# Two weight chunks first in the load queue of the first feature group

## The chip, the cores and the metric

The kernel runs on one core of one Trainium2 chip, in float32, in one launch. The metric is the device time in microseconds (us); the lower, the better. A core has TensorE (PE, matmuls; its loads of stationary operands are listed as PEld), VectorE (DVE), ScalarE (ACT), GpSimd (POOL) and SyncE (SP), which here only issues DMA transfers. They run side by side and wait for each other through semaphores.

## The reference

One layer of a decoder is computed for 288 tokens: 256 of a prompt and 8 requests of 4 tokens. `c` holds nine conditioning vectors, one for the prompt and one for each request.

```
mod = silu(c) @ w_ada + b_ada            # (9, 6 * 2048): sh1, sc1, g1, sh2, sc2, g2
h = rmsnorm(x, norm1) * (1 + sc1) + sh1
proj = h @ w_in                          # 2048 -> u_pool, z, xbc, dt
...                                      # pooling mixer, Mamba-2 mixer
x = x + g1 * (concat(pool_out, ssd_out) @ w_out)
h2 = rmsnorm(x, norm2) * (1 + sc2) + sh2
...                                      # gated MLP with a causal convolution
x = x + g2 * ffn_out
```

The change touches only the first part: `sh1` and `sc1`, the normalised and modulated input `h`, and the columns of the projection that are computed first.

## The kernel before

Features lie on the 128 partitions, tokens on the free axis (N = 288). The 2048 input features are KT = 16 feature tiles of 128.

**Feature groups.** The first projection can't start before `h` exists, and `h` needs `sh1` and `sc1`, a product with 2 x 2048 columns of `w_ada`. The kernel therefore splits the input features into six groups, `KGROUPS`, of 1, 1, 2, 4, 4 and 4 feature tiles (groups 0 to 5). For each group it first makes the conditioning (`ada_group_units`): 4, 4, 8, 16, 16 and 16 loads of 512 KB (`raw_ada`), which small matmuls consume in batches of four loads (tile `adag`), a copy on ACT (`asb_g`), a transposing matmul (`adat_g`), an addition on DVE (`ada`). Then `modulate` makes `h` for these feature tiles (`h_g`), casts it on ACT to a rounded high part (`h1h`, L368) and subtracts on DVE to a low part (`h1l`, L369).

**The projection.** `xbc_units(gi)` then adds this group's share to all ET = 28 output tiles, numbered `m` (i in the loop below). Its weights come in chunks of 512 KB (`raw_xbc`; the last chunk of groups 0 and 1 has 256 KB): 4, 4, 7, 14, 14 and 14 chunks in groups 0 to 5. A chunk holds 8 output tiles in groups 0 and 1, 4 in group 2, and 2 in groups 3 to 5. `split` casts a chunk on ACT to the high part `whi` (L220) and subtracts on DVE for the low part `wlo` (L221); there are two buffers of each. Three matmuls (L226 to L228) make each product from high and low parts. The result leaves PSUM by copies on ACT in group 0 (L574) and is added by DVE in the later groups (L576); three PSUM buffers rotate.

**The order of loads.** `load` (L213) takes one of 16 `raw` buffers and issues the transfer on SP's queue. All weights go through this one queue in program order, and a load whose buffer is not free holds up the ones behind it. The engines' own order is set by the framework's scheduler at build time; SP's order in the trace is that of the program.

**Interleaving.** `next_groups` is a generator that yields after each conditioning load; the call after a batch's fourth load also issues the batch's matmuls, and the call after a group's last load also its `modulate`. Before the loop over groups, `AN[0]` = 5 calls are made: group 1's four loads, and then group 1's matmuls and `modulate` with the first load of group 2. In the loop, `pull` adds a rate after each output tile and makes a call for each whole unit of credit:

```
    for _ in range(AN[0]):
        next(nxt)
...
        for i, m in enumerate(xbc_units(gi)):
            if not last:
                pull(nxt, AN[gi + 1] / (ET - 4))
```

A chunk's load stands where `xbc_units` reaches it, unless it is in `ready` already (before: only chunk 0 of group 0). `vec` (L895) is a table that is loaded at the start of group 1.

Of the kernel before, what the change touches and what calls it, by code (L numbers as in the profile page):

```python
# [35 lines left out]
ET = XT + len(UEARLY) + 3 * ZEARLY  # L36
# [4 lines left out]
YK = 2  # L41
AQ = (4, 4, 4, 4, 4, 4)

AN = (5, 5, 7, 11, 14, 15)
AY = 2

RA1, RA2, RB1, RB2, RB3 = 0.5, 0.4, 1.0, 1.0, 1.0
# [86 lines left out]
def kernel(ctx: ExitStack, tc, ins, outs):  # L134
# [75 lines left out]
    def load(key):  # L210
        off, cols = S.items[key]
        t = wp[0].tile([P, RAWC], F32, tag="raw", name="raw_" + "_".join(map(str, key)))
        nc.sync.dma_start(t[:, :cols], wflat[off:off + P * cols].rearrange("(p n) -> p n", p=P))  # L213
        return t

    def split(raw, a, n, name, urgent=True):
        hi = wp[0].tile([P, RAWC], F32R, tag="whi", name="whi_" + name)
        lo = wp[0].tile([P, RAWC], F32R, tag="wlo", name="wlo_" + name)
        with tc.high_priority() if urgent else nullcontext():
            nc.scalar.copy(hi[:, :n], raw[:, a:a + n])  # L220
            nc.vector.tensor_tensor(lo[:, :n], raw[:, a:a + n], hi[:, :n].bitcast(F32), ALU.subtract)  # L221
        return hi, lo

    def mm3(ps, whi, wlo, c, bh, bl, first, last, n=P):
        w = slice(c * n, c * n + n)
        nc.tensor.matmul(ps, whi[:, w], bh, start=first, stop=False)  # L226
        nc.tensor.matmul(ps, whi[:, w], bl, start=False, stop=False)  # L227
        nc.tensor.matmul(ps, wlo[:, w], bh, start=False, stop=last)  # L228

    ready = {}  # L230
# [223 lines left out]
    def late_loads():  # L454
        nc.vector.tensor_copy(selr, seli)
        nc.vector.tensor_scalar(csr, vec[:, K_TRI:K_TRI + N], 0.0, None, ALU.mult)

    def late_states():
        nc.sync.dma_start(poolw, ins["pool_w"])
        st = sx[0].tile([P, XT * NB * 3 + 4 * NB * 15], F32, tag="cf", name="st", bufs=2)  # L460
        nc.sync.dma_start(st, ins["st"])
        n = XT * NB * 3
        for g in range(4):
            nc.gpsimd.tensor_copy(cvs(g)[:, :, :, 0:3], st[:, 0:n].rearrange(
                "p (g m b l) -> p g m b l", g=4, m=5, b=NB)[:, g])
        nc.gpsimd.tensor_copy(ups.rearrange("p m b l -> p (m b) l")[:, :, 0:15],
                              st[:, n:].rearrange("p (m l) -> p m l", l=15))
# [86 lines left out]
    def xbc_units(gi):  # L554
        k0, gk = KGROUPS[gi]
        for ci, (ks, ms) in enumerate(_xbc_chunks(gi)):
            hi, lo = split(ready.pop(("xbc", gi, ci), None) or load(("xbc", gi, ci)), 0, len(ms) * gk * P, f"xbc{gi}_{ci}",
                           gi + 1 == len(KGROUPS))
            for b, m in enumerate(ms):
                ps = pm.tile([P, 512], F32, tag="mm", name=f"xbc{gi}_{m}")  # L560
                for i, k in enumerate(ks):
                    mm3(ps[:, :N], hi, lo, b * gk + i, xhi[0][k], xlo[0][k], i == 0, i == gk - 1)
                if m < XT:
                    g, r = divmod(m, 5)
                    parts = [(cvp[g][:, r, 3:3 + NP], ps[:, 0:NP]), (cvs(g)[:, r, :, 3:7], samp(ps[:, NP:N]))]
                elif m < XT + len(UEARLY):
                    u = UEARLY[m - XT]
                    parts = [(upp[:, u, 15:], ps[:, 0:NP]), (ups[:, u, :, 15:19], samp(ps[:, NP:N]))]
                else:
                    g, t = divmod(m - XT - len(UEARLY), 3)  # L570
                    parts = [(zy[g][:, t, :], ps[:, 0:N])]
                for o, v in parts:
                    if gi == 0:
                        nc.scalar.copy(o, v)  # L574
                    else:
                        nc.vector.tensor_tensor(o, o, v, ALU.add)  # L576
                yield m

    def drain(gen):
        for _ in gen:  # L580
            pass
# [253 lines left out]
    def next_groups():  # L835
        for gi in range(1, len(KGROUPS)):
            k0, gk = KGROUPS[gi]
            yield from ada_group_units(gi)
            modulate(xav(k0, gk), rstd1, 0, 0, k0, gk, f"g{gi}")

    nxt = next_groups()
# [29 lines left out]
    def pull(gn, rate):  # L871

        credit[id(gn)] = credit.get(id(gn), 0.0) + rate
        while credit[id(gn)] >= 1:
            credit[id(gn)] -= 1
            next(gn, None)

    ready["xbc", 0, 0] = load(("xbc", 0, 0))
    for _ in range(AN[0]):
        next(nxt)  # L880
    for gi in range(len(KGROUPS)):
        last = gi + 1 == len(KGROUPS)
        if last:

            wp[0].drop(w0)
            w0_ctx.close()
            sx[0] = mx_ctx.enter_context(tc.tile_pool(name="sx", bufs=1, reuse_waits="tile"))
            hi, lo = split(load(("dt",)), 0, KT * NH, "dt")
            ps = pm.tile([P, 512], F32, tag="mm", name="mm_dt")
            for k in range(KT):  # L890
                mm3(ps[0:NH, :N], hi, lo, k, xhi[0][k], xlo[0][k], k == 0, k == KT - 1, NH)
            late_states()
            dt_stage(ps)
        elif gi == 1:
            nc.sync.dma_start(vec, ins["vec"])  # L895
        elif gi == 4:
            late_loads()
        for i, m in enumerate(xbc_units(gi)):
            if not last:
                pull(nxt, AN[gi + 1] / (ET - 4))  # L900
                if i == ET - 4 and gi == 4:
                    drain(nxt)
            else:
                pull(back, 0.5 if m < 20 else RB1) if m >= 9 else None
                pull(adas, RA1 / AY)
# [389 lines left out]
```

## Time and profile before

| | |
|---|---|
| median of 3 runs | 1383.16 us (1382.48 to 1385.14) |
| the profiled execution, its time | 1382.64 us |
| its span in the trace | 1380.9 us |
| mean granted TensorE clock | 0.993 |
| TensorE busy | 1357.1 us (98%) |
| DVE busy | 822.1 us (60%) |
| ACT busy | 575.8 us (42%) |
| moved by DMA | 323.20 MB |

The span runs from the first to the last instruction of the program in the trace; the execution's own time is 1.7 us longer. Busy is the time in which an engine works on an instruction; the granted clock is a share of full speed, where 1.00 is 2.4 GHz.

### The profile page before, as it was taken

Reading aid. Unit: us, or ns where it says so; the run is one execution under the profiler, and the core shown is the slowest. Engines: PE = TensorE matmul, PEld = TensorE weight load, DVE = VectorE, ACT = ScalarE, POOL = GpSimd, SP = SyncE. Lnnn points to the kernel's source line nnn. Section 1 sums busy time; section 2 is a strip of 40 time slices with the busy share of each in tenths; the row PEclk is TensorE's granted clock in tenths of the full one; section 3 lists DMA queues with packets and bytes.
Section 4 is the critical chain, followed back from the end, with each engine's and each line's share of the span. In section 5 each row is a group of like instructions: output and inputs, shape, how many; then the busy total and the mean of one; then the engine's idle time right before and its main releaser. Section 6 shows DMA issues by size and latency. Waiting matters only on the chain.

```text
span 1380.9 us, 26414 instructions
## 1 busy us (share of the span) xinstructions
PE 1357.1 (98%) x10557; PEld 1256.4 (91%) x10557; DVE 822.1 (60%) x1450; ACT 575.8 (42%) x925; POOL 222.8 (16%) x426
## 2 busy tenths in 40 slices
PE   7899999999999999999999999999999999999997
PEld 6789887776679898998999999999999999999997
DVE  3686667977674448655655545665555556565553
ACT  3432334378653334533443333444343333443452
POOL 0000001222222123111211001222120012122221
PEclk9999999999999999999999999999999999999998
DMA  9997876888788877788655555655555555665531
GB/s 373 357 341 287 309 261 255 316 297 298 271 330 320 323 277 254 234 275 290 205 179 180 166 169 184 202 191 186 182 181 161 177 193 188 198 187 193 187 119 69
DMA packets 97194, 323.20 MB, mean 234 GB/s; under 512 B 10736, under 2 KB 19888, under 8 KB 97072
## 3 DMA queue, kind: packets, MB, share of 16 engines
q1 hardware_dynamic: 93168, 310.63, 65.2%
q0 software_dynamic: 3184, 9.69, 1.9%
q8 instruction: 83, 1.36, 0.4%
q10 hardware_dynamic: 720, 1.19, 0.2%
q14 instruction: 39, 0.32, 0.1%
HBM read 309.78 MB, written 10.39 MB: 232 GB/s over the span
## 4 chain that ended last, share of the span: by engine, by line
PE 94%; DVE 3%; DMA 1%; ACT 1%; issue 1%; POOL 0%; SPq 0%; DVEq 0%; ACTq 0%; POOLq 0%
PE mm_down L226 7%; PE mm_down L228 7%; PE mm_down L227 7%; PE mm_gate L228 6%; PE mm_gate L226 6%; PE mm_val L227 6%; PE mm_gate L227 6%; PE mm_val L228 6%; PE mm_val L226 6%; PE adap L255 4%; PE xbc L226 4%; PE xbc L228 4%; PE xbc L227 4%; PE mm_out L226 3%; PE mm_out L227 2%; PE mm_out L228 2%
## 5 line engine op out<-in xcount | busy, mean ns | idle before, releaser
L226 PE MATMUL mm_down<-ah,whi_down 128*128 128x288 f32 x688 | 203.7, 296 | 0.0
L228 PE MATMUL mm_down<-ah,wlo_down 128*128 128x288 f32 x688 | 203.5, 296 | 0.0
L227 PE MATMUL mm_down<-al,whi_down 128*128 128x288 f32 x688 | 203.3, 295 | 0.0
L228 PE MATMUL mm_gate<-h2h,wlo_gate 128*128 128x288 f32 x640 | 190.2, 297 | 0.0
L226 PE MATMUL mm_gate<-h2h,whi_gate 128*128 128x288 f32 x640 | 189.8, 297 | 0.0
L227 PE MATMUL mm_gate<-h2l,whi_gate 128*128 128x288 f32 x640 | 189.3, 296 | 0.0
L227 PE MATMUL mm_val<-h2l,whi_val 128*128 128x288 f32 x640 | 188.8, 295 | 0.0
L228 PE MATMUL mm_val<-h2h,wlo_val 128*128 128x288 f32 x640 | 188.5, 295 | 0.0
L226 PE MATMUL mm_val<-h2h,whi_val 128*128 128x288 f32 x640 | 188.0, 294 | 0.0
L221 DVE TENSOR_TENSOR wlo_gate<-raw_gate,whi_gate 128x1024 fp32r<-128x1024 f32 x80 | 97.9, 1225 | 139.4 <-ACT whi_gate L220 139.3
L221 DVE TENSOR_TENSOR wlo_down<-raw_down,whi_down 128x1024 fp32r<-128x1024 f32 x96 | 107.8, 1123 | 117.0 <-ACT whi_down L220 116.1
L220 ACT CAST whi_down<-raw_down 128x1024 fp32r<-128x1024 f32 x96 | 92.2, 961 | 168.6 <-PE mm_down L227 120.6
L220 ACT CAST whi_gate<-raw_gate 128x1024 fp32r<-128x1024 f32 x80 | 83.9, 1050 | 163.7 <-PE mm_gate L227 75.4
L226 PE MATMUL xbc<-h1h,whi_xbc 128*128 128x288 f32 x448 | 137.0, 307 | 6.9 <-ACT whi_xbc L220 3.4
L220 ACT CAST whi_val<-raw_val 128x1024 fp32r<-128x1024 f32 x80 | 84.1, 1051 | 123.3 <-issue 104.2
L227 PE MATMUL xbc<-h1l,whi_xbc 128*128 128x288 f32 x448 | 133.4, 298 | 0.4 <-DVE h1l L369 0.4
L228 PE MATMUL xbc<-h1h,wlo_xbc 128*128 128x288 f32 x448 | 132.4, 300 | 1.2 <-DVE wlo_xbc L221 0.9
L227 PEld LDWEIGHTS mm_down<-al,whi_down 128*128 128x128 f32 x688 | 129.7, 189 | 0.0
L228 PEld LDWEIGHTS mm_down<-ah,wlo_down 128*128 128x128 f32 x688 | 129.6, 188 | 0.0
L226 PEld LDWEIGHTS mm_down<-ah,whi_down 128*128 128x128 f32 x688 | 129.6, 188 | 0.0
L226 PEld LDWEIGHTS mm_gate<-h2h,whi_gate 128*128 128x128 f32 x640 | 120.4, 188 | 5.0 <-ACT ah L1060 3.4
L227 PEld LDWEIGHTS mm_gate<-h2l,whi_gate 128*128 128x128 f32 x640 | 120.7, 189 | 0.0
(318 smaller groups left out, 2994.4 us busy)
## 6 DMA issues: line engine op xcount, KB each, us to landing
raw_adap<-wflat SPq DMA_DIRECT2D x128, 512.0 KB, 6.0
raw_gate<-wflat SPq DMA_DIRECT2D x80, 512.0 KB, 3.6
raw_val<-wflat SPq DMA_DIRECT2D x80, 512.0 KB, 3.6
raw_ada<-wflat SPq DMA_DIRECT2D x64, 512.0 KB, 8.3
raw_xbc<-wflat SPq DMA_DIRECT2D x55, 512.0 KB, 6.8
raw_down<-wflat SPq DMA_DIRECT2D x48, 512.0 KB, 3.6
raw_out<-wflat SPq DMA_DIRECT2D x32, 512.0 KB, 7.8
raw_down<-wflat SPq DMA_DIRECT2D x32, 384.0 KB, 3.1
```

What stands on the lines that cost most here:

```text
L220: nc.scalar.copy(hi[:, :n], raw[:, a:a + n])
L221: nc.vector.tensor_tensor(lo[:, :n], raw[:, a:a + n], hi[:, :n].bitcast(F32), ALU.subtract)
L226: nc.tensor.matmul(ps, whi[:, w], bh, start=first, stop=False)
L227: nc.tensor.matmul(ps, whi[:, w], bl, start=False, stop=False)
L228: nc.tensor.matmul(ps, wlo[:, w], bh, start=False, stop=last)
L255: nc.tensor.matmul(ps[32 * j:32 * j + 32, :nb], sc_c[:, k, :], raw[:, c:c + nb], start=(k == 0), stop=(k == KT - 1), tile_position=(0, 32 ...
```

## The change

Two chunks of group 0 are loaded ahead of the five calls in place of one. The rates of the calls change: for groups 1 to 5 `AN[1:]` goes from 5, 7, 11, 14, 15 to 4, 9, 12, 16, 15, and a new tuple `AT` gives, for each group, the output tile from which calls are made at all: 10 in group 0, 0 in the others. The rate is now `AN[gi + 1]` over the tiles from there to ET - 4. In group 0 these calls are loads (and the first batch of matmuls) of group 2's conditioning.

```diff
-AN = (5, 5, 7, 11, 14, 15)
+AN = (5, 4, 9, 12, 16, 15)
+AT = (10, 0, 0, 0, 0)
...
-    ready["xbc", 0, 0] = load(("xbc", 0, 0))
+    for ci in range(2):
+        ready["xbc", 0, ci] = load(("xbc", 0, ci))
     for _ in range(AN[0]):
         next(nxt)
...
         for i, m in enumerate(xbc_units(gi)):
             if not last:
-                pull(nxt, AN[gi + 1] / (ET - 4))
+                if i >= AT[gi]:
+                    pull(nxt, AN[gi + 1] / (ET - 4 - AT[gi]))
                 if i == ET - 4 and gi == 4:
                     drain(nxt)
```

Order of the loads on SP's queue in group 0, from the first load of group 0's conditioning (a: conditioning, x: chunk; group, then number):

```
before: a0.0-3 x0.0 a1.0-3 a2.0 a2.1 x0.1 a2.2 a2.3 x0.2 a2.4 a2.5 x0.3 vec x1.0
after:  a0.0-3 x0.0 x0.1 a1.0-3 a2.0 a2.1 x0.2 a2.2 a2.3 x0.3 a2.4 a2.5 vec x1.0
```

## Rows read from the trace of the kernel before

**Rows 1.** The page: span, and each engine's busy time, share and instructions.

```profile
span 1380.9 us, 26414 instructions
...
PE 1357.1 (98%) x10557; PEld 1256.4 (91%) x10557; DVE 822.1 (60%) x1450; ACT 575.8 (42%) x925; POOL 222.8 (16%) x426
```

**Rows 2.** Stretches of 5 us: length, each engine's busy time, clock, DMA share, GB/s.

```profile
20.00:25.00 5.00, 3.37 (x22) 2.88 (x22) 2.96 (x6) 2.55 (x12) 0.00 (x0) 1.00 1.03 410
25.00:30.00 5.00, 2.98 (x71) 2.41 (x70) 0.76 (x3) 1.69 (x8) 0.64 (x2) 1.00 1.04 411
30.00:35.00 5.00, 3.50 (x11) 2.81 (x12) 2.95 (x3) 2.23 (x8) 0.00 (x0) 0.58 1.02 401
35.00:40.00 5.00, 5.00 (x80) 4.64 (x78) 0.88 (x1) 3.26 (x12) 0.00 (x0) 0.74 1.03 410
40.00:45.00 5.00, 4.80 (x33) 4.37 (x34) 1.34 (x4) 4.13 (x17) 0.00 (x0) 1.00 1.05 415
45.00:50.00 5.00, 4.22 (x79) 3.45 (x77) 2.60 (x7) 1.86 (x4) 0.00 (x0) 1.00 0.82 319
50.00:55.00 5.00, 4.35 (x33) 3.45 (x25) 4.20 (x15) 1.22 (x2) 0.40 (x1) 1.00 0.79 286
55.00:60.00 5.00, 3.08 (x32) 1.72 (x35) 4.62 (x13) 1.71 (x3) 0.36 (x2) 0.81 1.02 408
60.00:65.00 5.00, 5.00 (x35) 4.17 (x27) 3.85 (x16) 0.62 (x1) 0.00 (x0) 0.85 0.87 302
65.00:70.00 5.00, 5.00 (x55) 3.86 (x54) 4.74 (x13) 1.05 (x1) 0.00 (x0) 1.00 0.92 351
```

**Rows 3.** TensorE's waits, 0 to 160 us: for whom, total us, times, longest.

```profile
PE xbc L226 <- ACT whi_xbc L220: 3.4, 2, 2.7
PE xbc L226 <- DVE cvp L576: 1.9, 1, 1.9
```

**Rows 4.** TensorE's timeline, 20 to 62 us: start, length, instruction, idle before.

```profile
21.25 0.66 PE L226 MATMUL xbc<-h1h,whi_xbc 128*128 128x288 f32 x3 [1.22 <-ACT h1h L368]
...
25.59 1.95 PE L303 MATMUL adag<-raw_ada,sc_c 128*32 128x128 f32 x64
...
31.17 0.61 PE L226 MATMUL xbc<-h1h,whi_xbc 128*128 128x288 f32 x1 [2.75 <-ACT whi_xbc L220]
...
46.31 0.40 PE L226 MATMUL xbc<-h1h,whi_xbc 128*128 128x288 f32 x1 [0.65 <-ACT whi_xbc L220]
```

**Rows 5.** ACT's timeline, 20 to 62 and 60 to 95 us.

```profile
29.73 0.43 ACT L368 CAST h1h<-h_g 128x288 fp32r<-128x288 f32 x1 [1.80 <-POOL h_g L366]
30.07 1.04 ACT L220 CAST whi_xbc<-raw_xbc 128x1024 fp32r<-128x1024 f32 x1
...
66.49 1.05 ACT L220 CAST whi_xbc<-raw_xbc 128x1024 fp32r<-128x1024 f32 x1 [2.87 <-PE xbc L227]
...
93.88 1.05 ACT L220 CAST whi_xbc<-raw_xbc 128x1024 fp32r<-128x1024 f32 x1 [2.53 <-DMA raw_ada<-wflat]
```

**Rows 6.** SP's timeline, 0 to 62 us: the issues of loads.

```profile
7.80 7.02 SPq L213 DMA_DIRECT2D raw_ada<-wflat  x6
15.77 0.33 SPq L213 DMA_DIRECT2D raw_xbc<-wflat  x1
...
27.01 0.33 SPq L213 DMA_DIRECT2D raw_xbc<-wflat  x1
```

**Rows 7.** DMA issues, 15.7 to 16 us; the last number is us to landing.

```profile
raw_xbc<-wflat SPq DMA_DIRECT2D x1, 512.0 KB, 11.2
```

**Rows 8.** The same, 26.9 to 27.2 us.

```profile
raw_xbc<-wflat SPq DMA_DIRECT2D x1, 512.0 KB, 9.8
```

**Rows 9.** The same, 76.0 to 76.3 us, around an issue at 76.14.

```profile
raw_xbc<-wflat SPq DMA_DIRECT2D x1, 512.0 KB, 5.9
```

## The prediction, made before the change was run

> **What bounds the kernel now.** I began with the page. TensorE is busy for 98% of the span [rows 1], so time can come only from the rest, and the next view is the busy time of each engine in stretches of 5 us: where is TensorE idle, or slow? From 65 us on it is full at the full clock; the losses lie before that [rows 2]. From 20 to 45 us it is idle for 1.63 + 2.02 + 1.50 + 0.20 = 5.35 us, and from 45 to 60 us for 0.78 + 0.65 + 1.92 = 3.35 us. The granted clock is 0.58 and 0.74 from 30 to 40 us, and 0.81 and 0.85 from 55 to 65 us, which loses 0.42 x 5 + 0.26 x 5 = 3.4 us and 0.19 x 5 + 0.15 x 5 = 1.7 us. The waits tell by whom: 3.4 us for ACT's casts of weights, 1.9 us for VectorE's emptying of PSUM [rows 3].
>
> The timelines show the largest. TensorE ends the first chunk of group 0 at about 25.6 us, runs group 1's conditioning, and then stands 2.75 us before the second chunk's first matmul at 31.17, the clock at half just after [rows 4, 2]. On ACT the cast that it waits for, at 30.07, stands directly behind the cast of group 1's h1 (29.73), which waited for the conditioning chain [rows 5]. But the chunk itself was late as well: it was issued at 15.77, behind the six conditioning loads that begin at 7.80 [rows 6], and took 11.2 us to land [rows 7], thus at 26.95. Without the h1 cast it would have been cast at about 28.0.
>
> Over this stretch the DMA share is 1.02 to 1.05 up to 45 us [rows 2]: the early part is bound by how fast one queue delivers, and the order of that queue decides what TensorE can do meanwhile.
>
> **The change, part by part.** No transfer, matmul, cast or copy is added or removed: the edit permutes 122 loads on SP's queue and the points at which conditioning is pulled. I followed the loop by hand for both versions.
>
> *Group 0's loads.* Chunk 1 moves from the 12th place of the queue (counted from the first conditioning load) to the 6th, chunk 2 from the 15th to the 13th, chunk 3 from the 18th to the 16th. Group 1's four loads and group 2's first two slide back by one place. The rate start of 1/3.5 from tile 10 gives its first pull at tile 13 and still five pulls in group 0, so the same 18 loads and `vec` are ahead of group 1's first chunk, which stays the 20th. A place costs 512 KB at the 410 GB/s of those stretches, 1.28 us [rows 2]. Place 6 is now issued at 7.80, and chunk 1 should land six places before its 26.95, at about 19.3: before TensorE starts group 0 at 21.25 [rows 4]. Group 1's conditioning is late by one place, 1.28 us, and has until group 1's first matmul.
>
> *What TensorE can then do.* Between 21.25 and 46.31, where group 1's first matmul stands now [rows 4], it loses 5.35 + 0.65 - 1.25 = 4.75 us idle (the 1.25 before 21.25 stay) and 3.4 us to the clock. Its work is 25.06 - 4.75 - 3.4 = 16.9 us, and without these losses it would reach group 1 at 38.15. *What the queue allows:* group 1's first chunk is issued at 27.01 [rows 6] and lands 9.8 us later [rows 8], at 36.8; with ACT's cast of 1.05 us [rows 5] TensorE can start at about 38.0. Both limits agree on 38.1, and two limits that meet cost something: I add 0.9 us, most of one cast, and take 39.0. **Gain 46.3 - 39.0 = 7.3 us.** Bounds: 8.2 us with nothing lost, and 2.0 us if a wait of 2.75 us with the clock loss of 3.4 us comes back one chunk later.
>
> One rule of the Trainium skill can be weighed here. Rows 2 show 401 to 415 GB/s between 20 and 45 us. The page "DMA: Bandwidth & Descriptors", Specifications, gives a core's HBM limit as about 358 GB/s; by it, an estimate, a chunk would take 1.46 us, and a queue of 19 transfers would have delivered group 1's chunk 3.4 us later, at 40.3, for a gain of some 4 us in place of 7.3. The trace does not agree with that limit (the same page's section on the iDMA fabric lists 408.7 GB/s for one load stream alone, which does agree), and the sum goes by the trace.
>
> *Group 1 itself, 46.3 to 70 us.* TensorE loses 0.13 + 0.65 + 1.92 = 2.7 us idle and 1.7 us by the clock, so its work is 23.7 - 4.4 = 19.3 us. VectorE is busy 2.60 + 4.20 + 4.62 + 3.85 + 4.74 = 20.0 us there [rows 2]: both engines want nearly the same, and VectorE sets a floor of 20.0. The gain lies between 0 and 3.7 us. It depends on whether group 2's conditioning meets VectorE between two copies, as it does now at 54 to 57 us. The order of the copies isn't readable from here; group 2's loads finish at the same place of the queue, while pulls come more slowly in group 0 and faster in group 1. **I take 2.0 us.**
>
> *Later pulls.* From 7, 11 and 14 to 9, 12 and 16 over 24 tiles: conditioning is pulled earlier, and the chunks of groups 1 to 4 slide back by up to six places. I cost this at nothing, because TensorE is full from 65 us on, and chunks wait for the cast and not the cast for them. The cover is measurable. Group 3's first chunk is issued at 76.14, lands 5.9 us later [rows 9], 82.0, and is cast at 93.88 [rows 5]. After the change it is the 55th in place of the 52nd; with the queue running on at 1.28 us a place from 36.8, it lands at 36.8 + 35 x 1.28 = 81.6, and its cast is due at 93.9 - 9.3 = 84.6: 3.0 us to spare. Group 2's first chunk moves from the 33rd to the 34th, lands at 54.7, and its cast is due at 66.5 - 9.3 = 57.2: 2.5 us to spare. Without cover, three places would cost 3.8 us. DMA's idle share from 45 to 55 us, (0.18 + 0.21) x 5 = 1.95 us [rows 2], must then go as well, which earlier released buffers should do.
>
> Behind group 2 the kernel runs full, so what TensorE is ahead at 70 us it keeps. **Sum: 7.3 + 2.0 = 9.3 us.** The profiled execution took 1382.64 us (span 1380.9, 1.7 around it); 1382.64 - 9.3 = 1373.3. The median of the runs is 0.5 above that execution, so against the median: 1373.9.
>
> **The rivals.**
> *The same wait one chunk later.* ACT takes its work in order. If group 1's conditioning now runs behind sixteen tiles, the h1 cast may stand before the cast of chunk 2 as it stood before that of chunk 1. Then 2.75 us of idle time and up to 3.4 us of clock stay. For it: chunk 2 moves by only two places, to a landing at 28.2. Against: by then TensorE has a second chunk to run. Gain 2.0 + 2.0 = 4.0 us: 1379.2.
> *VectorE or the queue takes it all.* Groups 1 and 2 give back what group 0 gained: no spare 2.5 us, no gain in group 1 and buffers that come free late. Or the order on TensorE is not altered by the order of the loads. Then 1381 to 1385, no change. Against: the 20 us floor of VectorE still lies below the 23.7 that the stretch takes.
> *Slower: TensorE outruns the queue in groups 2 and 3.* With 9 us less lead, and one to five places lost in these groups, it waits before chunks that now lie ready. One wait of 2.75 us cost 2.75 + 3.4 = 6.15 us with the clock at its half level of 1.2 GHz behind it [rows 4, 2]; two such use up 9.3 us and turn the sign, three give 1383.2 - 9.3 + 18.5 = 1392. The point is a delivery of more than 2.5 us behind the 54.7 worked out above. Against it stands that DMA still has slack after 45 us. The Trainium skill speaks for this rival: "TensorE: Matmul & The Clock Gate", HAM oscillation, tells of short bursts between DMA waits that pay the half clock each time. By that rule, the trace agrees for the one wait that it has, and shows none from 65 us on.
>
> **How the numbers follow.** Forecast (gain 6 to 12 us) 0.66; the same wait a chunk later 0.17, still faster; no change 0.10; outrunning the queue 0.07. The predicted time is the forecast's, 1373.9. All bounds at their best give 8.2 + 3.7 = 11.9 us, 1371.3; the range goes 0.8 below that for small terms, and up to 1380.0, which takes in the second case and leaves out the last two. By the same cases, with 0.2% (2.8 us) as about what a measurement of this kernel can tell from no change: faster 0.83, same 0.10, slower 0.07.
>
> **What the profile will show.** Right: the second chunk's matmuls directly after the first's near 25.6 us; its cast before the h1 cast of group 1; a full clock from 25 to 45 us; group 1's first matmul at 38 to 40 us; DMA share near 1 through 45 to 55 us; TensorE full behind it. Wrong: a wait of over 2 us for a cast between 28 and 36 us (second case); waits for `raw_xbc` or a lowered clock between 55 and 100 us (last case); group 1 starting at 38 but 70 us reached no earlier (third).

## The result, and the profile after

The changed kernel takes 1386.93 us (median of 9 runs, 1385.55 to 1387.86) against 1383.34 us for the kernel before in the same comparison: a ratio of 1.0029 [1.002, 1.0037], slower by 3.6 us. The prediction was 9.3 us faster. The profiled execution has a span of 1384.3 us, 3.4 more than before. All code below the edit's first lines has moved down by one line: the matmuls are L227 to L229, the cast L221, the subtraction L222, the h1 cast L369, the copies L575, the additions L577.

The page, span and busy times:

```profile
span 1384.3 us, 26412 instructions
...
PE 1357.2 (98%) x10557; PEld 1256.9 (91%) x10557; DVE 821.2 (59%) x1450; ACT 576.0 (42%) x925; POOL 222.0 (16%) x426
```

All five busy times are within 1 us of [rows 1]: the work is the same, and TensorE does it later. Stretches of 5 us, with the columns of [rows 2]:

```profile
20.00:25.00 5.00, 3.65 (x23) 3.19 (x24) 3.74 (x7) 3.80 (x14) 0.00 (x0) 1.00 1.03 409
25.00:30.00 5.00, 5.00 (x87) 4.65 (x86) 0.00 (x0) 3.36 (x18) 0.00 (x0) 1.00 1.03 406
30.00:35.00 5.00, 2.21 (x13) 1.54 (x12) 3.24 (x6) 2.52 (x7) 0.64 (x2) 0.92 1.03 406
35.00:40.00 5.00, 4.39 (x17) 4.05 (x18) 0.93 (x2) 3.02 (x14) 0.00 (x0) 0.50 1.02 407
40.00:45.00 5.00, 4.53 (x79) 3.79 (x78) 0.55 (x3) 2.39 (x7) 0.00 (x0) 0.89 1.03 410
45.00:50.00 5.00, 3.39 (x28) 2.63 (x32) 3.12 (x9) 0.91 (x1) 0.00 (x0) 0.79 1.03 406
50.00:55.00 5.00, 5.00 (x74) 4.37 (x67) 2.16 (x10) 1.21 (x2) 0.00 (x0) 0.87 0.84 298
55.00:60.00 5.00, 4.29 (x46) 2.78 (x46) 4.58 (x13) 1.71 (x3) 0.77 (x2) 1.00 0.93 334
60.00:65.00 5.00, 3.02 (x16) 2.18 (x15) 4.51 (x15) 0.62 (x1) 0.00 (x0) 1.00 0.97 356
65.00:70.00 5.00, 4.93 (x52) 3.76 (x53) 3.58 (x14) 0.71 (x1) 0.00 (x0) 1.00 0.91 313
```

From 25 to 30 us TensorE is now full, as forecast, and from 30 to 35 us it loses 2.79 us. Over 20 to 45 us it is idle for 1.35 + 0 + 2.79 + 0.61 + 0.47 = 5.22 us (before 5.35), and the clock takes 0.08 x 5 + 0.50 x 5 + 0.11 x 5 = 3.45 us (before 3.4): the loss has moved, not shrunk. The same sum of this view from 45 to 110 us (the stretches behind 70 us are not printed) gives 6.10 us idle, before 3.35; the clock's loss there is 1.7 us in both. These 2.75 us are most of the 3.4 us by which the span grew.

TensorE's waits, 20 to 160 us (for whom: total us, times, longest):

```profile
PE xbc L229 <- DVE wlo_xbc L222: 3.9, 7, 0.9
PE xbc L227 <- ACT whi_xbc L221: 3.9, 2, 2.4
PE xbc L227 <- DVE cvp L577: 1.9, 3, 1.1
```

The waits for ACT's casts have not gone (3.4 us in two before, [rows 3]), and those for the subtractions on VectorE cost 3.9 us in seven. In the kernel before they were this line of the same view:

```profile
PE xbc L228 <- DVE wlo_xbc L221: 0.9, 2, 0.6
```

TensorE's timeline, beside [rows 4]:

```profile
20.95 0.66 PE L227 MATMUL xbc<-h1h,whi_xbc 128*128 128x288 f32 x3 [1.21 <-ACT h1h L369]
...
27.88 1.95 PE L304 MATMUL adag<-raw_ada,sc_c 128*32 128x128 f32 x64
...
33.45 0.40 PE L227 MATMUL xbc<-h1h,whi_xbc 128*128 128x288 f32 x1 [2.43 <-ACT whi_xbc L221]
35.53 1.09 PE L229 MATMUL xbc<-h1h,wlo_xbc 128*128 128x288 f32 x3 [0.89 <-DVE wlo_xbc L222]
...
45.96 0.40 PE L227 MATMUL xbc<-h1h,whi_xbc 128*128 128x288 f32 x1 [1.43 <-ACT whi_xbc L221]
```

Between 20.95 and 31 us there is no wait for chunk 1. Then the wait of 2.75 us of before stands before chunk 2, with 2.43 us, and 0.89 us more for the low part, at half the clock. Group 1 starts at 45.96 instead of 46.31. ACT's timeline says what the cast stood behind:

```profile
32.02 0.43 ACT L369 CAST h1h<-h_g 128x288 fp32r<-128x288 f32 x1 [0.50 <-POOL h_g L367]
32.36 1.04 ACT L221 CAST whi_xbc<-raw_xbc 128x1024 fp32r<-128x1024 f32 x1
...
44.86 1.05 ACT L221 CAST whi_xbc<-raw_xbc 128x1024 fp32r<-128x1024 f32 x1
52.29 0.27 ACT L261 COPY asb_g<-adag 128x128 f32<-128x128 f32 x1 [6.38 <-PE adag L304]
52.45 1.05 ACT L221 CAST whi_xbc<-raw_xbc 128x1024 fp32r<-128x1024 f32 x1
```

At 32.36 the cast of chunk 2 is directly behind group 1's h1 cast, as that of chunk 1 was in [rows 5]. At 52.45 the cast of group 1's second chunk is behind a conditioning copy, before which ACT stood idle for 6.38 us; before the change it stood behind the same copy, at 50.36. Neither was late as a load. SP's issues:

```profile
5.58 2.27 SPq L214 DMA_DIRECT2D raw_xbc<-wflat  x2
...
16.76 0.33 SPq L214 DMA_DIRECT2D raw_xbc<-wflat  x1
...
26.09 0.33 SPq L214 DMA_DIRECT2D raw_xbc<-wflat  x1
```

and, with the columns of [rows 7], the issue at 16.76 (chunk 2):

```profile
raw_xbc<-wflat SPq DMA_DIRECT2D x1, 512.0 KB, 10.5
```

Chunk 2 landed at 16.76 + 10.5 = 27.3, 5.1 us before its cast. Group 1's second chunk, issued at 30.60, landed at 40.8.

### The profile page after: what moved, and what is told of

It is laid out like the page before. It is cut to its first block, busy times and chain, and to the rows that moved or that the text cites. A ratio compares the mean times of both kernels' runs of the same rounds, so it can differ in the third digit from the quotient of the medians.

```text
span 1384.3 us, 26412 instructions
## 1 busy us (share of the span) xinstructions
PE 1357.2 (98%) x10557; PEld 1256.9 (91%) x10557; DVE 821.2 (59%) x1450; ACT 576.0 (42%) x925; POOL 222.0 (16%) x426
## 4 chain that ended last, share of the span: by engine, by line
PE 94%; DVE 4%; issue 1%; DMA 1%; ACT 0%; POOL 0%; SPq 0%; DVEq 0%; POOLq 0%; ACTq 0%
PE mm_down L229 7%; PE mm_down L227 7%; PE mm_down L228 7%; PE mm_gate L229 6%; PE mm_gate L227 6%; PE mm_val L228 6%; PE mm_gate L228 6%; PE mm_val L229 6%; PE mm_val L227 6%; PE adap L256 4%; PE xbc L227 4%; PE xbc L229 4%; PE xbc L228 4%; PE mm_out L227 3%; PE mm_out L228 2%; PE mm_out L229 2%
## 5 line engine op out<-in xcount | busy, mean ns | idle before, releaser
L227 PE MATMUL mm_down<-ah,whi_down 128*128 128x288 f32 x688 | 203.8, 296 | 0.0
L229 PE MATMUL mm_down<-ah,wlo_down 128*128 128x288 f32 x688 | 203.7, 296 | 0.0
L229 PE MATMUL mm_gate<-h2h,wlo_gate 128*128 128x288 f32 x640 | 190.4, 298 | 0.0
L227 PE MATMUL mm_gate<-h2h,whi_gate 128*128 128x288 f32 x640 | 189.9, 297 | 0.0
L229 PE MATMUL mm_val<-h2h,wlo_val 128*128 128x288 f32 x640 | 188.7, 295 | 0.0
L227 PE MATMUL mm_val<-h2h,whi_val 128*128 128x288 f32 x640 | 188.2, 294 | 0.0
L222 DVE TENSOR_TENSOR wlo_gate<-raw_gate,whi_gate 128x1024 fp32r<-128x1024 f32 x80 | 98.1, 1230 | 139.3 <-ACT whi_gate L221 138.3
L222 DVE TENSOR_TENSOR wlo_down<-raw_down,whi_down 128x1024 fp32r<-128x1024 f32 x96 | 108.2, 1127 | 116.9 <-ACT whi_down L221 116.1
L221 ACT CAST whi_down<-raw_down 128x1024 fp32r<-128x1024 f32 x96 | 92.2, 960 | 168.4 <-PE mm_down L228 122.0
L221 ACT CAST whi_gate<-raw_gate 128x1024 fp32r<-128x1024 f32 x80 | 83.7, 1049 | 163.2 <-PE mm_gate L228 68.1
L227 PE MATMUL xbc<-h1h,whi_xbc 128*128 128x288 f32 x448 | 137.1, 307 | 7.6 <-ACT whi_xbc L221 3.9
L229 PE MATMUL xbc<-h1h,wlo_xbc 128*128 128x288 f32 x448 | 132.1, 302 | 4.3 <-DVE wlo_xbc L222 4.3
L221 ACT CAST whi_val<-raw_val 128x1024 fp32r<-128x1024 f32 x80 | 84.1, 1051 | 120.6 <-issue 101.6
L229 PEld LDWEIGHTS mm_down<-ah,wlo_down 128*128 128x128 f32 x688 | 129.8, 189 | 0.0
L227 PEld LDWEIGHTS mm_down<-ah,whi_down 128*128 128x128 f32 x688 | 129.7, 189 | 0.0
L227 PEld LDWEIGHTS mm_gate<-h2h,whi_gate 128*128 128x128 f32 x640 | 120.6, 188 | 5.0 <-ACT ah L1063 3.4
```

## The experiments

Diffs are against the changed kernel; each ratio is against the kernel before. The edit has three parts: how many chunks go first (one or two; some runs have three), the pause (`AT[0]` = 10 with `AN[1]` = 4, without it 0 and 5), and the three rates (7, 11, 14 or 9, 12, 16). "Idle" is TensorE's idle time from the 5-us view, as above. A group's length runs from its first projection matmul to that of the next group.

Two cautions. Each comparison has its own median for the kernel before, 1382.2 to 1383.3 us, so ratios compare better than medians. And a trace is one execution: group 0 took 25.0 us in the changed kernel's, and 24.9 and 27.1 in those of e18 and e8, whose edits begin behind it; in e8 the clock was at 0.81 and 0.85 from 20 to 30 us, in the other two it was full. Group 1's start in two traces thus compares to within about 2 us.

**Two chunks first, nothing else** (e1)

```diff
-AN = (5, 4, 9, 12, 16, 15)
-AT = (10, 0, 0, 0, 0)
+AN = (5, 5, 7, 11, 14, 15)
+AT = (0, 0, 0, 0, 0)
```

> Two chunks first, with the old rates and no pause. Theory A: the loss of the full change, 3.6 us, is made in group 2 by the higher rates, which put group 3's modulate on VectorE ahead of the remaining subtractions; the load order alone only moves the wait from chunk 1 to chunk 2. Then this run takes 1381 to 1385 us, no change, and group 2's start to group 3's start takes about 29 us as before. Theory B: the load order does the harm (later chunks come late): 1386 to 1387 us.

1380.36 us, 0.9976 [0.9967, 0.9985]: faster than before, and below the ranges of both theories. Chunk 2's cast still stands behind the h1 cast, but the wait is 1.01 us, the clock stays full from 30 to 40 us, and group 1 starts at 43.35.

**The rates alone** (e2)

```diff
-AN = (5, 4, 9, 12, 16, 15)
-AT = (10, 0, 0, 0, 0)
+AN = (5, 5, 9, 12, 16, 15)
+AT = (0, 0, 0, 0, 0)
...
-    for ci in range(2):
+    for ci in range(1):
```

> Old order of loads and no pause, with the new rates 9, 12, 16. Theory A: 1386 to 1388 us, with VectorE waits in group 2 (subtractions of chunks 5 and 6 behind group 3's modulate) and group 3 starting some 4 us later than before. Theory B: 1382 to 1385 us, no change.

1385.14 us, 1.0013 [1.0004, 1.0022]: the rates alone cost 0.13%, between the two theories. Idle from 45 to 110 us is 5.33 us. What theory A names is in the trace: TensorE's waits for subtractions rise from 0.9 to 3.0 us, and group 2 takes 32.0 us in place of 28.95.

**The change with the old rates** (e3)

```diff
-AN = (5, 4, 9, 12, 16, 15)
+AN = (5, 4, 7, 11, 14, 15)
```

> The full change with its pause, but the old rates 7, 11, 14 in the later groups. Theory A: 1381 to 1385 us, the loss gone. Theory B: 1386 to 1388 us, the loss stays.

1381.99 us, 0.9992 [0.9983, 1.0001]. Idle from 45 to 110 us is 3.26 us, against the 6.10 of the change, but TensorE waits 2.44 us for chunk 2 and group 1 starts only at 47.2: by the medians the pause, added to e1, took back two thirds of what the two chunks had brought.

**The casts of group 0 at high priority** (e4). The argument decides for which groups the scheduler is asked to put a chunk's cast and subtraction first.

```diff
-                           gi + 1 == len(KGROUPS))
+                           gi in (0, len(KGROUPS) - 1))
```

> The full change, with casts and subtractions of group 0's chunks given priority over other work on ACT and VectorE. Theory A2: chunk 2 was landed at 27.3 us and its cast stood only behind the h1 cast on ACT; with the cast first the wait of 2.4 us and the half clock behind it go, group 1 starts at 40 to 42 us in place of 46.0, and with the loss in group 2 still there the time is 1381 to 1383 us. Rival: the wait is taken over by another one (h1 of group 1 late, the cast of group 1's first chunk late) and group 1 starts at 45 us or later, 1386 to 1388 us.

1387.13 us, 1.0026 [1.0017, 1.0035]. ACT's order did not change; chunk 2's cast was still behind the h1 cast. The edit did not do what it was for, so it tells nothing of the theory.

**The change without the pause** (e7)

```diff
-AN = (5, 4, 9, 12, 16, 15)
-AT = (10, 0, 0, 0, 0)
+AN = (5, 5, 9, 12, 16, 15)
+AT = (0, 0, 0, 0, 0)
```

> The full change without its pause: two chunks first, new rates 9, 12, 16, calls from tile 0 of group 0. Theory A, in two parts: the pause takes away the conditioning batch that fills TensorE's wait for chunk 2, and the rates cost some 4 us in group 2. Then group 1 starts near 43.3 us, as with the old rates and no pause, group 3 some 2 us later than before, and the time is 1383 to 1385 us. Rival: the pause is harmless and the rates alone make the whole loss: 1386 to 1388 us.

1382.02 us, 0.999 [0.9982, 0.9999], 4.9 us less than the change and 1 us below theory A's range. TensorE's timeline shows what the pause had removed:

```profile
29.54 1.95 PE L304 MATMUL adag<-raw_ada,sc_c 128*32 128x128 f32 x64
...
32.62 1.96 PE L304 MATMUL adag<-raw_ada,sc_c 128*32 128x128 f32 x64
35.58 0.40 PE L227 MATMUL xbc<-h1h,whi_xbc 128*128 128x288 f32 x1 [1.01 <-ACT whi_xbc L221]
```

The second batch is the first of group 2's conditioning. It fills most of the wait for chunk 2; what is left is 1.01 us in place of 2.43, and group 1 starts at 44.05. In the changed kernel the same batch runs at 40.59, behind the wait.

**Group 3's modulation held back to output tile 24 of group 2** (e8)

```diff
+    held = []
...
-            modulate(xav(k0, gk), rstd1, 0, 0, k0, gk, f"g{gi}")
+            if gi == 3:
+                held.append(lambda: modulate(xav(4, 4), rstd1, 0, 0, 4, 4, "g3"))
+            else:
+                modulate(xav(k0, gk), rstd1, 0, 0, k0, gk, f"g{gi}")
...
+                if gi == 2 and i == 24:
+                    held.pop()()
```

> The full change, but group 3's modulate (multiplications, cast, subtractions) is held back to tile 24 of group 2, while its loads and conditioning stay where the change puts them. Theory A: the loss in group 2 is VectorE's order, 3 us of modulate ahead of the subtractions of chunks 5 and 6; then TensorE's waits for wlo_xbc between 90 and 100 us go, group 3 starts at about 100 us, and the time is 1382.5 to 1385 us. Rival: the loss is the queue's (the chunks come later behind the earlier conditioning loads): group 3 still starts at 103 us or later and the time is 1386 to 1388 us.

1388.03 us, 1.0037 [1.0024, 1.005]; idle from 45 to 110 us is 7.16 us, no less than without this edit. The loss moved: group 2 takes 30.7 us in place of the change's 32.2, but group 3 takes 56.7 in place of 54.95, with a wait of 0.97 us for a subtraction near its start. Holding the modulation back is no cure; that its place costs group 2 some 1.6 us, the trace does show.

**The pause alone** (e9)

```diff
-AN = (5, 4, 9, 12, 16, 15)
+AN = (5, 4, 7, 11, 14, 15)
...
-    for ci in range(2):
+    for ci in range(1):
```

> The pause alone: one chunk first as before, old rates, calls in group 0 from tile 10. Theory A: the pause costs by itself, since group 2's first batch of conditioning is not there to fill waits: group 1 starts 1 to 3 us later than before, 1383.5 to 1386.5 us. Rival: the pause is neutral or frees the queue for chunks 1 and 2, 1380 to 1383 us.

1378.19 us, 0.9966 [0.9954, 0.9979]. This was not expected, and lies below both ranges: with one chunk first the pause gains 0.34%, with two (e1 to e3) it loses 0.16%. Here it takes conditioning loads from ahead of chunks 1 and 2: chunk 1 landed at 25.2, its cast at 28.64 stands ahead of the h1 cast at 31.41, and the wait before it is 0.51 us. From 45 to 110 us TensorE is idle for 1.83 us and loses nothing by the clock.

**Three chunks first, nothing else** (e10)

```diff
-AN = (5, 4, 9, 12, 16, 15)
-AT = (10, 0, 0, 0, 0)
+AN = (5, 5, 7, 11, 14, 15)
+AT = (0, 0, 0, 0, 0)
...
-    for ci in range(2):
+    for ci in range(3):
```

> Three chunks first, old rates, no pause. In this kernel's order on ACT the cast of chunk 2 stands ahead of group 1's h1 cast. Theory A2 (the wait of 2.4 us for chunk 2 is ACT's order): no wait of over 1 us for a cast between 28 and 36 us, group 1 starts at 39 to 41.5 us, 1376 to 1380 us. Rival: group 1's conditioning, one place later still, or its first chunk takes the wait over: group 1 at 43 us or later, 1380 to 1384 us.

1379.04 us, 0.9974 [0.9965, 0.9983]. Chunk 2's cast is now ahead of the h1 cast, there is no wait for it, and group 1 starts at 41.90, as theory A2 said to within 0.4 us.

**Each chunk of groups 0 to 2 issued one chunk earlier** (e11)

```diff
+    asked = {("xbc", 0, 0), ("xbc", 0, 1)}
...
+            nk = ("xbc", gi, ci + 1) if ci + 1 < len(_xbc_chunks(gi)) else ("xbc", gi + 1, 0)
+            if nk[1] < 3 and nk not in ready and nk not in asked:
+                ready[nk] = load(nk)
+                asked.add(nk)
```

> The full change, with each chunk of groups 0 to 2 issued one chunk earlier: directly behind the split of the chunk before the one that it follows, so that it stands some three places further ahead in SP's queue. Theory (the new rates cost because they put more conditioning loads ahead of each chunk, so the order fixed at build time places its cast and subtraction later): TensorE's idle time from 45 to 110 us falls from 6.1 to 3.3 us or less, chunk 2's cast stands ahead of group 1's h1 cast, group 1 starts at 43 us or earlier, and the time is 1379 to 1381. Rival (the conditioning's own work, its copies and additions, takes the place of the subtractions on VectorE): the idle time there stays at 4.7 to 7, only group 0 gains, and the time is 1382 to 1385.

1382.82 us, 1.0 [0.9991, 1.0008]. In group 0 chunk 2 landed at 26.2, 1.1 us earlier than in the change, and its cast at 31.57 stands ahead of the h1 cast at 32.92; the wait for it is 0.76 us, and group 1 starts at 40.8. Group 2 starts at 61.7 us, 8.4 ahead of the kernel before (about 1.8 of it a conditioning batch that has moved from group 1 into group 2). That is nearly the 9.3 of the prediction, and the kernel gives all of it back: idle from 45 to 110 us is 7.02 us, with these waits in that stretch, and the longest of them in TensorE's timeline:

```profile
PE xbc L227 <- DVE cvp L583: 4.6, 5, 2.6
PE xbc L229 <- DVE wlo_xbc L222: 2.4, 3, 1.2
```

```profile
89.79 0.37 PE L227 MATMUL xbc<-h1h,whi_xbc 128*128 128x288 f32 x1 [2.58 <-DVE cvp L583]
```

VectorE's timeline shows what the additions stood behind:

```profile
85.97 1.65 DVE L360 TENSOR_SCALAR h_g<-h_g,amul,ada 128x256 f32<-128x256 f32 x4
87.65 1.56 DVE L370 TENSOR_TENSOR h1l<-h_g,h1h 128x288 fp32r<-128x288 f32 x4
89.13 0.51 DVE L583 TENSOR_TENSOR cvp<-cvp,xbc 128x256 f32<-128x256 f32 x2
```

Group 3's modulation and low part, 3.2 us, run there in one piece. The theory's sign was right for group 0 alone; the rival's was right behind it.

**Three chunks first, pause, old rates** (e12)

```diff
-AN = (5, 4, 9, 12, 16, 15)
+AN = (5, 4, 7, 11, 14, 15)
...
-    for ci in range(2):
+    for ci in range(3):
```

> Three chunks first, with the pause, and the rates of before (5, 4, 7, 11, 14, 15): the kernel with three chunks first (1379.0) plus the pause alone. Theory (the pause costs only because it takes away the conditioning batch with which TensorE fills its wait for chunk 2; with chunk 2 ahead there is no such wait): within 1 us of the kernel with three chunks first, 1378 to 1380, group 1 starts at 41 to 43 us. Rival (the pause costs by itself wherever more than one chunk is first, as it cost 1.6 us with the old rates and two chunks): 1380.5 to 1382.5, with more idle time from 45 to 70 us, where the second group's conditioning now has to be done.

1376.87 us, 0.996 [0.9946, 0.9973]: the fastest kernel of this study, and 1.1 us below what the theory gave. By the medians the pause, which lost with two chunks, gains 2.2 us here (e10 to e12); the intervals overlap, so what is clear is that it does not cost. ACT's timeline shows the casts of chunk 2 and of group 1 ahead of the conditioning that they stood behind in the changed kernel:

```profile
26.46 1.06 ACT L221 CAST whi_xbc<-raw_xbc 128x1024 fp32r<-128x1024 f32 x1
...
34.94 0.43 ACT L369 CAST h1h<-h_g 128x288 fp32r<-128x288 f32 x1 [0.23 <-POOL h_g L367]
...
40.85 2.00 ACT L221 CAST whi_xbc<-raw_xbc 128x1024 fp32r<-128x1024 f32 x2
47.76 0.27 ACT L261 COPY asb_g<-adag 128x128 f32<-128x128 f32 x1 [4.91 <-PE adag L304]
```

The cast at 26.46 is chunk 2's, 8.5 us ahead of the h1 cast; the two at 40.85 are the first chunks of group 1, 7 us ahead of the copy. Stretches of the same kernel, with the clock full where the changed kernel has 0.92 and 0.50:

```profile
30.00:35.00 5.00, 5.00 (x87) 4.61 (x86) 0.76 (x3) 2.78 (x14) 0.64 (x2) 1.00 1.03 406
35.00:40.00 5.00, 4.63 (x84) 4.04 (x83) 2.81 (x5) 3.41 (x12) 0.00 (x0) 1.00 1.02 408
```

**The later two rates only, two chunks, no pause** (e14)

```diff
-AN = (5, 4, 9, 12, 16, 15)
-AT = (10, 0, 0, 0, 0)
+AN = (5, 5, 7, 12, 16, 15)
+AT = (0, 0, 0, 0, 0)
```

> Two chunks first, no pause, and of the three new rates only the two later ones: 7 in group 1 as before, 12 in group 2 and 16 in group 3. It stands between two kernels that were run: old rates 1380.4, all new rates 1382.0. Theory (the loss is made in group 1, where VectorE is busy for 20.0 of 24 us and a rate of 9 in place of 7 adds two more loads' conditioning): 1380 to 1381, idle from 45 to 110 us near 2.6. Rival (it is made in groups 2 and 3, where group 2 takes 32 us with the new rates against 29): 1381.7 to 1383, idle 4.5 or more, group 3's start at 100 us against 97.

1385.69 us, 1.0019 [1.0011, 1.0028], outside what either theory gave: slower than e1 and also than e7, between which it stands. Two rates cost more here than all three. Idle from 45 to 110 us is 4.19 us, and group 3 starts at 99.6 against 97.0 in e1; 3.4 us are lost by group 5's start (213.5 against 210.1), and the rest is lost behind it, where no cause was sought.

**The change with three chunks first** (e6)

```diff
-    for ci in range(2):
+    for ci in range(3):
```

> The full change with three chunks first in place of two. Theory (two separate losses: the wait for chunk 2 in group 0, and the new rates in groups 1 and 2): group 0's wait of 2.43 us and the half clock behind it go, group 1 starts at 42.5 us or earlier, but the idle time from 45 to 110 us stays at 4.5 to 7 us, and the time is 1381 to 1384. Rival (the later waits follow from group 0's late start and go with it): idle there under 3.5 us and 1378 to 1380.

1379.44 us, 0.9975 [0.9966, 0.9983]: one more chunk ahead turns the change from 0.29% slower to 0.25% faster. Group 1 starts at 42.7; idle from 45 to 110 us is 3.81 us, between the two, but the time is the rival's: group 1 starts 3.2 us earlier than in the change and takes 22.4 us in place of 25.0, at the full clock in place of 0.79 and 0.87. Group 2 takes the same 32.2 us in both: the later loss in group 1 went with the wait in group 0, that in group 2 stayed. Against e12 the new rates still cost 2.6 us of medians.

**The rates one by one, three chunks first with the pause** (e15, e16)

```diff
-AN = (5, 4, 9, 12, 16, 15)
+AN = (5, 4, 9, 11, 14, 15)
...
-    for ci in range(2):
+    for ci in range(3):
```

and for e16 the same with `AN = (5, 4, 7, 12, 16, 15)`.

> Three chunks first, with the pause, and of the three new rates only group 1's: (9, 11, 14). It stands between 1376.9 (7, 11, 14) and 1379.4 (9, 12, 16). Theory (the loss is made in group 1, where VectorE has the least room): 1378.8 to 1380, and idle time from 45 to 110 us near 3.8 us. Rival (it is made in groups 2 and 3): 1376.4 to 1377.6, idle near 2.4 us.

> Three chunks first, with the pause, and of the three new rates only the later two: (7, 12, 16). Theory (the loss is made in group 1): 1376.4 to 1377.6. Rival (it is made in groups 2 and 3): 1378.8 to 1380. If this and the run with group 1's rate alone both come out above 1378.8 or both below 1377.6, the rates do not act one by one, and the loss belongs to the order that comes out as a whole.

1378.21 us, 0.9966 [0.9953, 0.9978], and 1377.54 us, 0.9963 [0.995, 0.9975], both between e12 and e6, with idle of 3.24 and 3.39 us. By the medians group 1's rate costs 1.3 us here and the later two 0.7, but the intervals overlap with each other and with e12's: no one rate is the culprit. Group 2 takes 30.8 and 30.5 us against 27.2 in e12, with one conditioning batch more in it.

**The subtractions of groups 1 and 2 on GpSimd** (e18)

```diff
-            nc.vector.tensor_tensor(lo[:, :n], raw[:, a:a + n], hi[:, :n].bitcast(F32), ALU.subtract)
+            (eng or nc.vector).tensor_tensor(lo[:, :n], raw[:, a:a + n], hi[:, :n].bitcast(F32), ALU.subtract)
...
-                           gi + 1 == len(KGROUPS))
+                           gi + 1 == len(KGROUPS), nc.gpsimd if gi in (1, 2) else None)
```

> The full change, with the subtractions for the low parts of groups 1 and 2 (11 chunks) moved from VectorE to GpSimd, which is busy for 16% of the span. Theory (VectorE is late with them, since the faster pulls put the conditioning's additions and modulation ahead of them): the waits for the low part after 45 us, 3.9 us in 7, fall to under 1 us, idle from 45 to 110 us from 6.1 to 3.5 us or less, and the time by 2 to 3 us, to 1384 to 1385; the wait for chunk 2 in group 0 stays. Rival (the order as a whole is at fault, or GpSimd is too slow for a chunk of 1024 columns, which TensorE uses up in 3.2 us): the waits move to the casts or to PSUM, or grow, and the time is 1386 to 1392.

1390.48 us, 1.0059 [1.0045, 1.0072]; idle from 45 to 110 us rose to 8.99 us. The waits in that stretch:

```profile
PE xbc L227 <- ACT whi_xbc L221: 3.9, 2, 2.4
PE xbc L227 <- DVE cvp L577: 3.0, 5, 1.6
PE xbc L229 <- POOL wlo_xbc L222: 1.4, 1, 1.4
PE xbc L229 <- DVE amul L271: 1.0, 1, 1.0
PE xbc L229 <- DVE wlo_xbc L222: 0.4, 1, 0.4
```

The matmul that takes the low part (L229) waits for 1.4 + 1.0 + 0.4 = 2.8 us in place of 3.0 in the same stretch of the changed kernel, and the waits for casts and PSUM grew. GpSimd takes about 2.4 us for a chunk (2.39 is the median of the 11, and the profile's spans on GpSimd are rough) and VectorE 1.22, so the test is not a clean one; it does not bear out that VectorE's load by itself is what the rates cost.

**One load moved** (e19 on the change, e20 on the kernel before, e21 on e1). The fast kernels e9 and e12 have the cast of group 1's second chunk ahead of the conditioning copy, the changed kernel has it behind.

```diff
         for ci, (ks, ms) in enumerate(_xbc_chunks(gi)):
...
+            if (gi, ci) == (1, 0):
+                ready["xbc", 1, 1] = load(("xbc", 1, 1))
```

> The full change with one load moved: group 1's second chunk is issued directly behind the split of its first one, ahead of the conditioning loads between them. That puts its cast ahead of group 2's conditioning copy on ACT; chunk 2's cast in group 0 stays behind the h1 cast. Theory (the loss behind group 0 is mostly this one cast): it runs at 46 to 47 us in place of 52.45, idle from 45 to 110 us falls from 6.1 to under 4.3 us, the clock's loss there from 1.7 to 0, and the time by 2 to 4 us, to 1383 to 1385. Rival (the new rates cost by themselves, wherever this cast stands): idle stays above 5 us, and the time is 1386 to 1388.

> The kernel before (one chunk first, no pause, old rates) with the same one load moved. Theory: the wait of 1.9 us for PSUM at 57 us and the clock's loss of 1.7 us behind it go, since VectorE has this chunk's subtraction behind it when group 2's conditioning comes: 2 to 4 us less, 1379 to 1381, group 2 starts at 66 to 68 us in place of 70.1. Rival (the wait goes elsewhere, since the subtractions and additions are the same): 1382 to 1384.

> Two chunks first, no pause, old rates (1380.4), with the same one load moved. Theory: as in the kernel before, 2 to 4 us less, 1376.5 to 1378.5, with the clock's loss of 3.4 us from 45 to 110 us gone. Rival: no change, 1379.5 to 1381.

1387.41 us, 1.0043 [1.0029, 1.0057]; 1382.86 us, 1.0008 [0.9999, 1.0016]; 1380.52 us, 0.9992 [0.9983, 1]. None gained; all three lie in their rivals' ranges. ACT's timeline of e19 shows that the cast did move (the second of the two at 46.14), 7 us ahead of the copy that it had stood behind:

```profile
46.14 2.00 ACT L221 CAST whi_xbc<-raw_xbc 128x1024 fp32r<-128x1024 f32 x2
54.32 0.27 ACT L261 COPY asb_g<-adag 128x128 f32<-128x128 f32 x1 [6.18 <-PE adag L304]
```

Idle from 45 to 110 us is 7.42 us, no less than the change's 6.10. The theory fell: that cast's place goes along with the fast kernels and is not what makes them fast. Group 1 takes 23.6 us in e19, 1.4 less than in the change, and group 2 33.5, 1.2 more. In e3, which starts group 1 at the same 47.2 with the old rates, they take 22.5 and 27.2; of the 6.3 us in group 2, 1.8 are a conditioning batch that e3 does later.

The parts in one table (us; the last column has the ratios to before, old rates and then new):

| first | pause | old rates | new rates | ratios |
|---|---|---|---|---|
| one | no | 1383 (before) | 1385.1 | 1; 1.0013 |
| one | yes | 1378.2 | not run | 0.9966; - |
| two | no | 1380.4 | 1382.0 | 0.9976; 0.999 |
| two | yes | 1382.0 | 1386.9 (the change) | 0.9992; 1.0029 |
| three | no | 1379.0 | not run | 0.9974; - |
| three | yes | 1376.9 | 1379.4 | 0.996; 0.9975 |

## Why the prediction was wrong

Forecast was a gain of 7.3 us before group 1, 2.0 in it and nothing behind it. In the two traces the changed kernel is 0.35 us ahead at group 1's first matmul (45.96 against 46.31), 0.9 behind at group 2's (70.98 against 70.09), 4.2 behind at group 3's (103.22 against 99.04), 2.7 behind at group 5's (214.8 against 212.1), where all of this conditioning is done in both, and 3.4 behind at the end.

**Chunk 1's landing: right.** Forecast at about 19.3, measured 18.0; it was cast at 20.80 and followed chunk 0 without a wait. The cast stood before group 1's h1 cast, as the prediction said it would.

**The 7.3 us before group 1: the step that failed.** It was the sum of every loss between 21.25 and 46.31, as though chunk 1's lateness caused all of them, with two limits "that meet" at 38.1. The queue's limit held: group 1's first chunk, issued at 26.09, landed at 35.7, 1.1 us before the forecast 36.8. TensorE's did not. Its gain was 46.31 - 45.96 = 0.35 us. The bound was neither TensorE's work nor the queue but the order on ACT: chunk 2, landed at 27.3, was cast at 32.36 behind an h1 cast that waits for the conditioning chain. Three chunks first put that cast ahead of the h1 cast and group 1's start at 41.9 to 42.7 (e10, e12, e6); in e11, with chunk 2's landing only 1.1 us earlier, it is at 40.8. So the wait goes with the order on ACT, although no run moved the cast alone: each moved its load as well, and e4, which was to move the cast only, did not. The first rival named this mechanism and this place, with a chance of 0.17, but sized it wrong: it left 2.0 us of gain. The wait of 2.43, the 0.89 for the low part, the 1.43 before group 1 and 3.45 us by the clock used up all of it.

**The pause: not priced at all.** The working followed its loads on the queue and not the matmuls that its calls issue. Group 2's first batch, 1.96 us of TensorE's time, is what fills the wait for chunk 2 where there is no pause. With it taken away the clock fell as well, to 0.50 from 35 to 40 us: with the new rates the pause costs 4.9 us of medians (e7 to the change), with the old ones 1.6 (e1 to e3). Where the chunk that TensorE needs at that point is cast ahead of the h1 cast, it gains (chunk 1 in e9) or does not cost (chunk 2 in e12). That two parts, each good alone, undo each other is the larger part of the sign: 0.9976 x 0.9966 is 0.9942, and together (e3) they measured 0.9992, some 6.9 us more.

**Group 1's own gain of 2.0 us: a loss.** From group 1's first matmul to group 2's, the trace shows 71.0 - 45.96 = 25.0 us, before 23.8. The 1.7 us by the clock are in both; the waits for additions are 1.9 us in both, and those for subtractions 1.4 in place of 0.6. The bounds, 0 to 3.7, had no loss in them, although the prediction called the order of the copies there not readable. With the same rates and three chunks first (e6) the group takes 22.4 us.

**Later pulls at nothing: wrong.** The reasons given were that TensorE is full from 65 us on and that the queue has slack. The slack was real for group 2: its first chunk landed at 52.9 (forecast 54.7) and was cast only at 69.3. Group 3's first chunk landed at 87.4, 5.8 us behind the forecast and 2.8 behind the 84.6 at which the forecast had its cast; the cast came at 99.4, so that cover was not tested. But the price was not on the queue. In all four pairs of the table the new rates cost, between 0.13% and 0.37% of the time (from e1 to e7 and from e12 to e6 the intervals overlap), and TensorE's waits for subtractions from 20 to 110 us go up with them: 0.9 to 3.0 us from before to e2, 1.4 to 2.7 from e1 to e7, 1.3 to 2.5 from e12 to e6, 2.1 to 3.9 from e3 to the change.

The place where they cost is the same in all four pairs: group 2. It takes 28.95 us with the old rates and no pause (before, e1, e10), 27.2 with the old rates and the pause (e3, e9, e12), where it has one conditioning batch fewer, some 1.8 us, and 32.0 to 32.2 with the new rates (e2, e7, e6, the change). At the same conditioning that is 3.1 us more without the pause and 3.3 with it, whatever goes first; some of it comes back in group 3, which has a batch more and takes only 0.7 to 1.5 us longer. Only from e3 to the change does group 1 lengthen clearly as well, from 22.5 to 25.0 us. In the change about half of the loss shows as waits (1.6 us for subtractions) and the rest as longer busy time of TensorE. VectorE's timeline shows a difference in order. Before, the subtractions of group 2's last two chunks run ahead of group 3's modulation:

```profile
88.20 1.22 DVE L221 TENSOR_TENSOR wlo_xbc<-raw_xbc,whi_xbc 128x1024 fp32r<-128x1024 f32 x1
...
89.76 1.22 DVE L221 TENSOR_TENSOR wlo_xbc<-raw_xbc,whi_xbc 128x1024 fp32r<-128x1024 f32 x1
...
94.38 1.57 DVE L359 TENSOR_SCALAR h_g<-h_g,amul,ada 128x256 f32<-128x256 f32 x4
```

In the changed kernel they run behind it, and TensorE waits for the first of them:

```profile
91.50 1.48 DVE L360 TENSOR_SCALAR h_g<-h_g,amul,ada 128x256 f32<-128x256 f32 x4
92.90 1.55 DVE L370 TENSOR_TENSOR h1l<-h_g,h1h 128x288 fp32r<-128x288 f32 x4
...
95.33 1.22 DVE L222 TENSOR_TENSOR wlo_xbc<-raw_xbc,whi_xbc 128x1024 fp32r<-128x1024 f32 x1
...
99.00 1.22 DVE L222 TENSOR_TENSOR wlo_xbc<-raw_xbc,whi_xbc 128x1024 fp32r<-128x1024 f32 x1
```

```profile
96.60 0.40 PE L229 MATMUL xbc<-h1h,wlo_xbc 128*128 128x288 f32 x1 [0.67 <-DVE wlo_xbc L222]
```

Holding the modulation back (e8) shortened group 2 by 1.6 us and lengthened group 3 by 1.75. The chunks' place in the queue (e11), the place of one cast (e19) and VectorE's load (e18, not a clean test) were each tried as the cause, and none accounts for the loss; nor do the rates add up one by one with two chunks first (e14). The edit re-makes the order of all engines from there on. That the loss lies in group 2 is shown; how much of it the modulation's place makes, and whether another order avoids it, stays open.

**The rivals.** "TensorE outruns the queue" was right in sign, and its two waits would give 1383.2 - 9.3 + 12.3 = 1386.2, close to the measured time; but that is luck, since no wait for a load is among TensorE's, and from 20 to 45 us DMA ran at 406 to 410 GB/s (before 401 to 415). "VectorE or the queue takes it all" gave 1381 to 1385, and TensorE's waits in group 2 are for VectorE, but group 0 had gained nothing that could be given back; e11 is the kernel that did what it describes. Of the signs of being wrong that the prediction named, the first, "a wait of over 2 us for a cast between 28 and 36 us", is what the trace shows.

## What to carry to other kernels

When a wait is removed by an earlier load, look at what stands in front of the next cast on its engine: an engine takes its work in an order fixed at build time, and a load that landed 5 us ahead of its cast did not help, since the cast stood behind a waiting one. Before work is held back from a stretch, look whether it is what fills a wait there, and price its matmuls as well as its loads. Test the parts of such an edit singly and in pairs: here two parts that gain 0.24% and 0.34% alone gain 0.08% together, which is not clear of noise, and with the third part lose 0.29%. And compare a stretch of the work, such as one group, across all the variants: that showed where the rates cost when the totals did not.

## What the runs showed of the hardware that was not expected

The subtraction of 128x1024 elements took GpSimd about 2.4 us and VectorE 1.22 us, and the slower engine's spare time was no help (e18, 1390.48 us). The same group 0 ran at a granted clock of 0.81 and 0.85 from 20 to 30 us in one execution (e8) and at the full clock in two others (the change, e18). A conditioning batch (x64 in the trace) takes 1.95 us at the full clock and took 2.90 us at 49.32 in the changed kernel, where the granted clock of the stretches around it is 0.79 and 0.87.
